# Prefix logsumexp over time: two consecutive steps per partition, result over x, Exp one tile ahead, one table set

## The chip, the core and the metric

The kernel runs on one core of a Trainium2 chip. The core has five engines that run side by side and wait for each other through semaphores: TensorE (PE, matrix products), VectorE (DVE), ScalarE (ACT, functions such as Exp and Ln by tables), GpSimd (POOL) and SyncE (SP). In this kernel SP issues the loads and POOL the stores; all of them run on the same 16 DMA engines. The metric is device time in microseconds, the median of several runs of the same program.

## The reference

```python
def setup_inputs():
    B, S, D = (4, 4096, 4128)
    return {'x': np.random.randn(B, S, D).astype(np.float32)}

def reference(x):
    out[:, 0, :] = x[:, 0, :].copy()
    for t in range(1, S):
        mx = np.maximum(out[:, t - 1, :], x[:, t, :])
        out[:, t, :] = mx + np.log(np.exp(out[:, t - 1, :] - mx) + np.exp(x[:, t, :] - mx))
```

For each of four batches and each of 4128 columns this is a running logsumexp over 4096 time steps: out[t] = ln(exp(x[0]) + ... + exp(x[t])). Input and output are 270.5 MB each in float32.

## The kernel before

The kernel takes Exp of x, sums along time, and takes Ln of the sums. Time lies on the partitions: a tile is 128 consecutive time steps by all 4128 columns, 2.11 MB, and there are 32 tiles per batch, 128 in all. The loop over tiles (lines 54 and 55) is written straight down, and a scheduler sets the order of each engine's instructions from the loop and from the buffers that are free.

For each tile: SP loads xt (line 57; five buffers). ACT writes et = Exp(xt) in float16 (line 60; three buffers). The columns are then worked off in four chunks of 1024 and a tail of 32. For a chunk, PE multiplies et by the upper triangular matrix ut (line 69), which gives the running sums within the tile, in two matmuls of 512 columns; and it adds the running sum of the tiles before with a second pair of matmuls (line 74), whose matrix sel32 has 32 rows and picks the last row of the 32 rows of carry. ACT writes Ln of the sums to ot (line 79; four buffers), and DVE copies the last 32 rows of the sums in float16 to ncarry (line 82), the carry of the next tile. The chunks share three PSUM buffers (pmain); the tail has its own (ptail). POOL stores ot (line 93).

Three things set the order around the change. Each engine runs its instructions in order. The DVE copy of a chunk comes after ACT's Ln of the same chunk, and frees the PSUM buffer. Exp and Ln are taken from two different table sets, so ACT loads a table ahead of each Exp and again ahead of the Ln that follow.

Of the kernel before, what the change touches and what calls it, by code (L numbers as in the profile page):

```python
# [1 line left out]

# [5 lines left out]


@with_exitstack  # L10
def kernel(
    ctx: ExitStack,
    tc: tile.TileContext,
    x: bass.AP,
    out: bass.AP,
):
    nc = tc.nc
    fp32 = mybir.dt.float32
    fp16 = mybir.dt.float16

    B, S, D = x.shape
    P = 128
    n_tt = S // P
    assert S % P == 0

    MAIN = 1024
    MM = 512
    n_main = D // MAIN
    tail = D - n_main * MAIN
    half = (D // 2 + 3) & ~3  # L30

    consts = ctx.enter_context(tc.tile_pool(name="consts", bufs=1))
    ut = consts.tile([P, P], fp16)
    make_upper_triangular(nc, ut, val=1.0, diag=True)
    sel32 = consts.tile([32, P], fp16)
    nc.gpsimd.memset(sel32, 0.0)  # L36
    nc.gpsimd.affine_select(  # L37
        out=sel32, in_=sel32, pattern=[[0, P]],
        compare_op=mybir.AluOpType.not_equal, fill=1.0,
        base=-31, channel_multiplier=1,  # L40
    )

    xpool = ctx.enter_context(tc.tile_pool(name="xpool", bufs=5))
    epool = ctx.enter_context(tc.tile_pool(name="epool", bufs=3))
    opool = ctx.enter_context(tc.tile_pool(name="opool", bufs=4))
    cpool = ctx.enter_context(tc.tile_pool(name="cpool", bufs=3))
    psum_main = ctx.enter_context(tc.tile_pool(name="psum_main", bufs=3, space=bass.MemoryType.PSUM))
    psum_tail = ctx.enter_context(tc.tile_pool(name="psum_tail", bufs=2, space=bass.MemoryType.PSUM))

    carry = [None] * B  # L50

    for b in range(B):
        for k in range(n_tt):
            rows = slice(k * P, (k + 1) * P)

            xt = xpool.tile([P, D], fp32)
            nc.sync.dma_start(out=xt, in_=x[b, rows, :])

            et = epool.tile([P, D], fp16)
            nc.scalar.activation(et, xt, mybir.ActivationFunctionType.Exp)  # L60

            ot = opool.tile([P, D], fp32)
            ncarry = cpool.tile([32, D], fp16)

            def scan_chunk(pt, cols, width):
                for s in range(0, width, MM):
                    w = min(MM, width - s)
                    seg = slice(cols.start + s, cols.start + s + w)
                    nc.tensor.matmul(  # L69
                        pt[:, s:s + w], lhsT=ut, rhs=et[:, seg],  # L70
                        start=True, stop=(k == 0),
                    )
                    if k > 0:
                        nc.tensor.matmul(  # L74
                            pt[:, s:s + w], lhsT=sel32,
                            rhs=carry[b][0:32, seg],
                            start=False, stop=True,
                        )
                nc.scalar.activation(  # L79
                    ot[:, cols], pt[:, :width], mybir.ActivationFunctionType.Ln  # L80
                )
                nc.vector.tensor_copy(ncarry[0:32, cols], pt[96:128, :width])  # L82

            for c in range(n_main):
                pmain = psum_main.tile([P, MAIN], fp32)
                scan_chunk(pmain, slice(c * MAIN, (c + 1) * MAIN), MAIN)
            if tail:
                ptail = psum_tail.tile([P, tail], fp32)
                scan_chunk(ptail, slice(n_main * MAIN, D), tail)

            carry[b] = ncarry

            nc.gpsimd.dma_start(out=out[b, rows, :], in_=ot)  # L93


# [1 line left out]
_INS = ['x']  # L97
_OUTS = [((4, 4096, 4128), 'float32')]


# [23 lines left out]
```

## Time and profile before

| what | value |
|---|---|
| median of 3 runs (lowest to highest) | 1530.63 us (1530.13 to 1531.21) |
| profiled execution, first to last instruction | 1528.0 us |
| difference of that span and the median | 2.6 us |
| busy: ACT, PE, DVE | 1302.7, 1107.2, 620.6 us |
| DMA: bytes, mean rate over the span | 541.52 MB, 354 GB/s |
| of these: read and written by the kernel | 270.53 MB each |

The span runs from the first to the last instruction of one profiled execution; all durations below are from that execution, so a time worked out from them is a span, and stands 2.6 us under the median of the runs. "Busy" is time in which an engine executes; an engine can be busy while another sets the pace. The chain of work that ended last follows, from the last instruction back, what each step waited for. A DMA share is the mean share of time in which the 16 DMA engines had a packet under way, and the rate beside it says what they moved.

### The profile page before, as it was taken

What the parts mean: (1) busy time and instruction counts of PE and PEld (TensorE: products, weight loads), DVE (VectorE), ACT (ScalarE), POOL (GpSimd) and SP (SyncE); (2) the same over time, 40 slices, a digit from 0 to 9 for tenths busy, and PEclk for the clock granted to TensorE, in tenths of its full rate; (3) what the DMA queues carried; (4) which work ended last, traced back from release to release, by engine and by line L of the source; (5) the groups of instructions that cost most, each with busy time, mean ns of one, the idle gap of its engine ahead of it and who ended that gap; (6) DMA issues with size and microseconds to landing.
All of it is one profiled execution on the core that took longest, in us unless ns stands there. A gap on an engine that the chain in (4) does not pass through costs nothing.

```text
span 1528.0 us, 7011 instructions
## 1 busy us (share of the span) xinstructions
PE 1107.2 (72%) x2268; PEld 210.5 (14%) x2268; DVE 620.6 (41%) x640; ACT 1302.7 (85%) x1024; POOL 69.2 (5%) x136
## 2 busy tenths in 40 slices
PE   4767777677677776777767777777677777776776
PEld 1111111111111111111111111111111111111111
DVE  2334443444344433443344334433444344434444
ACT  8988888888988888888888888888889888888884
POOL 0000000000000000000000000000000000000000
PEclk7555555555555555555555555555555555555555
DMA  9999999999999999999999999999999999999945
GB/s 396 432 398 360 351 359 360 355 357 353 381 356 357 353 363 352 358 351 366 357 373 352 366 354 357 347 365 359 355 354 381 353 361 352 360 361 352 341 194 221
DMA packets 36900, 541.52 MB, mean 354 GB/s; under 512 B 4096, under 2 KB 4096, under 8 KB 4096
## 3 DMA queue, kind: packets, MB, share of 16 engines
q1 hardware_dynamic: 18432, 270.54, 53.9%
q0 software_dynamic: 18432, 270.54, 41.3%
q8 instruction: 17, 0.28, 0.1%
q14 instruction: 19, 0.16, 0.0%
HBM read 270.53 MB, written 270.53 MB: 354 GB/s over the span
## 4 chain that ended last, share of the span: by engine, by line
ACT 56%; PE 19%; issue 15%; DVE 10%; DMA 1%; ACTq 0%; DVEq 0%
ACT et L60 30%; ACT L60 11%; DVE ncarry L82 10%; ACT ot L79 10%; PE pmain L69 10%; PE pmain L74 9%; ACT L79 5%; DMA xt<-in_x_dram 1%; ACTq L60 0%; DVEq L119 0%; PE ptail L74 0%
## 5 line engine op out<-in xcount | busy, mean ns | idle before, releaser
L82 DVE CAST ncarry<-pmain 32x1024 f16<-32x1024 f32 x512 | 606.4, 1220 | 900.2 <-ACT ot L79 900.2
L69 PE MATMUL pmain<-et,ut 128*128 128x512 f16 x1024 | 613.6, 603 | 403.5 <-DVE ncarry L82 385.6
L79 ACT ACTIVATE ot<-pmain 128x1024 f32<-128x1024 f32 x512 | 496.6, 1024 | 199.3 <-PE pmain L74 195.1
L74 PE MATMUL pmain<-ncarry,sel 32*128 32x512 f16 x992 | 597.5, 602 | 0.0
L60 ACT ACTIVATE et<-xt 128x4128 f16<-128x4128 f32 x128 | 466.2, 3642 | 7.8 <-DMA xt<-in_x_dram 6.4
L74 PEld LDWEIGHTS <-sel 32*128 32x128 f16 x1116 | 101.0, 99 | 835.7 <-issue 835.7
L69 PEld LDWEIGHTS <-ut 128*128 128x128 f16 x1152 | 109.4, 104 | 471.6 <-issue 469.0
L60 ACT ACT_TABLE_LOAD x128 | 164.2, 1283 | 7.2 <-PE pmain L69 3.1
L79 ACT ACT_TABLE_LOAD x128 | 164.2, 1283 | 2.3
L93 POOL DMA_DIRECT2D out_dram<-ot x128 | 68.1, 532 | 1450.4 <-ACT ot L79 1450.4
L69 PE MATMUL ptail<-et,ut 128*128 128x32 f16 x128 | 26.2, 205 | 7.7 <-ACT et L60 7.7
L74 PE MATMUL ptail<-ncarry,sel 32*128 32x32 f16 x124 | 28.3, 228 | 0.0
L79 ACT ACTIVATE ot<-ptail 128x32 f32<-128x32 f32 x128 | 27.9, 218 | 0.0
L82 DVE CAST ncarry<-ptail 32x32 f16<-32x32 f32 x128 | 23.3, 182 | 0.0
masks.py:66 POOL TENSOR_SCALAR_AFFINE_SELECT ut<-ut 128x128 f16<-128x128 f16 x1 | 0.3, 282 | 0.1
L37 POOL TENSOR_SCALAR_AFFINE_SELECT sel<-sel 32x128 f16<-32x128 f16 x1 | 0.3, 282 | 0.0
masks.py:65 POOL MEMSET ut<- 128x128 f16 x1 | 0.2, 204 | 0.3 <-POOLq L108 0.3
L36 POOL MEMSET sel<- 32x128 f16 x1 | 0.2, 195 | 0.0
L108 POOL MEMSET const-float32-0.0<- 128x1 f32 x1 | 0.1, 103 | 0.2 <-issue 0.2
L108 POOL MEMSET const-bfloat16-1.0<- 128x1 bf16 x1 | 0.1, 106 | 0.0
L108 POOL MEMSET const-uint8-127<- 128x1 uint8 x1 | 0.1, 106 | 0.0
L108 POOL MEMSET const-float32-1.0<- 128x1 f32 x1 | 0.1, 103 | 0.0
## 6 DMA issues: line engine op xcount, KB each, us to landing
xt<-in_x_dram SPq DMA_DIRECT2D x128, 2064.0 KB, 11.3
out_dram<-ot POOLq DMA_DIRECT2D x128, 2064.0 KB, 12.1
```

What stands on the lines that cost most here:

```text
L36: nc.gpsimd.memset(sel32, 0.0)
L37: nc.gpsimd.affine_select(out=sel32, in_=sel32, pattern=[[0, P]], compare_op=mybir.AluOpType.not_equal, fill=1.0, base=-31, channel_multip ...
L60: nc.scalar.activation(et, xt, mybir.ActivationFunctionType.Exp)
L69: nc.tensor.matmul(pt[:, s:s + w], lhsT=ut, rhs=et[:, seg], start=True, stop=(k == 0),)
L74: nc.tensor.matmul(pt[:, s:s + w], lhsT=sel32, rhs=carry[b][0:32, seg], start=False, stop=True,)
L79: nc.scalar.activation(ot[:, cols], pt[:, :width], mybir.ActivationFunctionType.Ln)
L82: nc.vector.tensor_copy(ncarry[0:32, cols], pt[96:128, :width])
L93: nc.gpsimd.dma_start(out=out[b, rows, :], in_=ot)
L108: nc = _bacc.Bacc("TRN2", target_bir_lowering=False, num_devices=1)
```

## The change

A tile is now 256 consecutive time steps: partition p holds the steps 2p and 2p + 1, one after the other, so a tile is 4.23 MB and there are 64. Four 128x128 matrices in float16 take the place of ut and sel32: incl (rows up to and including), excl (rows before), ident, and last (the last row for all). For a chunk, `head` sums for the even steps: incl times the even rows, excl times the odd rows, last times the carry; ACT takes Ln of it. Then `second` adds ident times the odd rows into the same PSUM buffer, which makes it the sum at the odd steps; ACT takes Ln of that, and DVE copies all 128 rows to the carry of this chunk. The order is written out by hand (`manual_schedule`): `second` of chunk c - 1 comes after `head` of chunk c, and Exp of the next tile is issued ahead of the whole scan of a tile. Ln writes its result over x in xt, and the store reads xt; xt has five buffers of twice the size, et two. One table set that has both Exp and Ln is loaded once.

```diff
+    nc.scalar.preload_act_table_set("natural_log_exp_and_others")
...
     xpool = ctx.enter_context(tc.tile_pool(name="xpool", bufs=5))
-    epool = ctx.enter_context(tc.tile_pool(name="epool", bufs=3))
-    opool = ctx.enter_context(tc.tile_pool(name="opool", bufs=4))
-    cpool = ctx.enter_context(tc.tile_pool(name="cpool", bufs=3))
...
+    epool = ctx.enter_context(tc.tile_pool(name="epool", bufs=2))
+    cpool = ctx.enter_context(tc.tile_pool(name="cpool", bufs=1))
+    pmain = ctx.enter_context(tc.tile_pool(name="pmain", bufs=3, space=bass.MemoryType.PSUM))
...
+        def head(c):
+            pt = pmain.tile([P, CH], FP32, name="pt")
+            for s in range(0, CH, MM):
...
+                mm(o, incl, et[:, 0, seg], True, False)
+            for s in range(0, CH, MM):
...
+                mm(o, excl, et[:, 1, seg], False, first)
+            if not first:
+                for s in range(0, CH, MM):
+                    mm(pt[:, s:s + MM], last, carry[c][:, s:s + MM], False, True)
+            nc.scalar.activation(xt[:, 0, c * CH:(c + 1) * CH], pt, ACT.Ln)
+            return pt
...
+        def second(c, pt):
+            for s in range(0, CH, MM):
+                seg = slice(c * CH + s, c * CH + s + MM)
+                mm(pt[:, s:s + MM], ident, et[:, 1, seg], False, True)
+            nc.scalar.activation(xt[:, 1, c * CH:(c + 1) * CH], pt, ACT.Ln)
+            nc.vector.tensor_copy(carry[c], pt)
...
+        for c in range(n_main):
+            pt = head(c)
+            if prev is not None:
+                second(c - 1, prev)
+            prev = pt
...
+        second(n_main - 1, prev)
+        if tail:
+            nc.scalar.activation(xt[:, :, t0:D], qt, ACT.Ln)
+            nc.vector.tensor_copy(carry_t, qt[:, 1, :])
+        nc.gpsimd.dma_start(
+            out=out[b, k * rows:(k + 1) * rows, :].rearrange("(p j) d -> p j d", j=R), in_=xt,
+        )
...
+    for b, k in work:
+        xt = xpool.tile([P, R, D], FP32, name="xt")
+        nc.sync.dma_start(
+            out=xt, in_=x[b, k * rows:(k + 1) * rows, :].rearrange("(p j) d -> p j d", j=R),
+        )
+        et = epool.tile([P, R, D], FP16, name="et")
+        nc.scalar.activation(et, xt, ACT.Exp)
+        if pending is not None:
+            scan(*pending)
+        pending = (b, k, xt, et)
+    scan(*pending)
```

The same on ACT, for one tile in the middle of the program before (waits in brackets name the engine or the DMA whose semaphore is waited for):

```order
L60 ACT_TABLE_LOAD [waits DMAHW4_49]
L60 ACTIVATE et<-xt 128x4128 [waits PE_49]
L79 ACT_TABLE_LOAD
L79 ACTIVATE ot<-pmain 128x1024 [waits PE_49] x3
L79 ACTIVATE ot<-ptail 128x32 [waits DMASW7_49,PE_49,Activation_49]
L79 ACTIVATE ot<-pmain 128x1024 [waits PE_49]
L60 ACT_TABLE_LOAD [waits DMAHW5_49]
```

And for one tile of the program now, from its neighbour's Exp to the end of its scan (line 98 is Ln of `head`, line 105 Ln of `second`, line 124 the tail):

```order
L139 ACTIVATE et<-xt 128x8256 [waits DMAHW2_49]
L98 ACTIVATE xt<-pt 128x1024 [waits PE_49,Activation_49]
L98 ACTIVATE xt<-pt 128x1024 [waits PE_49]
L105 ACTIVATE xt<-pt 128x1024 [waits PE_49]
L98 ACTIVATE xt<-pt 128x1024 [waits PE_49]
L105 ACTIVATE xt<-pt 128x1024 [waits PE_49]
L98 ACTIVATE xt<-pt 128x1024 [waits PE_49]
L105 ACTIVATE xt<-pt 128x1024 [waits PE_49] x2
L124 ACTIVATE xt<-qt 128x2x32
```

The table loads are gone, the Exp is one instruction for two time steps per partition, and the eight Ln alternate between two chunks. The Exp at the top belongs to the tile after the one whose Ln follow.

On PE, a piece of the program before (numbers tell buffers apart; pmain_2328 is one chunk, ut and sel32 are the two matrices):

```order
L69 LDWEIGHTS ut_58
L69 MATMUL pmain_2328<-et_2310,ut_58 128x512 [waits DVE_49]
L74 LDWEIGHTS sel32_63
L74 MATMUL pmain_2328<-ncarry_2273,sel32_63 128x512
L69 LDWEIGHTS ut_58
L69 MATMUL pmain_2328<-et_2310,ut_58 128x512
L74 LDWEIGHTS sel32_63
L74 MATMUL pmain_2328<-ncarry_2273,sel32_63 128x512
```

And of the program now, at the end of `head` of chunk 1 (pt_289), `second` of chunk 0 (pt_281), and the start of `head` of chunk 2 (pt_301):

```order
L80 LDWEIGHTS last_70
L80 MATMUL pt_289<-carry1_91,last_70 128x512
L80 LDWEIGHTS ident_65
L80 MATMUL pt_281<-et_217,ident_65 128x512 [waits Activation_49]
L80 LDWEIGHTS ident_65
L80 MATMUL pt_281<-et_217,ident_65 128x512
L80 LDWEIGHTS incl_59
L80 MATMUL pt_301<-et_217,incl_59 128x512 [waits DVE_49]
L80 LDWEIGHTS incl_59
L80 MATMUL pt_301<-et_217,incl_59 128x512
```

Each matrix now serves two matmuls in a row, each with its own weight load. The matmul of `second` waits for ACT, and what stands behind it on PE waits with it.

## Rows read from the trace of the kernel before

**Rows 1.** Busy time of each engine, share of the span, instructions.
```profile
PE 1107.2 (72%) x2268; PEld 210.5 (14%) x2268; DVE 620.6 (41%) x640; ACT 1302.7 (85%) x1024; POOL 69.2 (5%) x136
```

**Rows 2.** The chain that ended last, shares of the span by line.
```profile
ACT et L60 30%; ACT L60 11%; DVE ncarry L82 10%; ACT ot L79 10%; PE pmain L69 10%; PE pmain L74 9%; ACT L79 5%; DMA xt<-in_x_dram 1%; ACTq L60 0%; DVEq L119 0%; PE ptail L74 0%
```

**Rows 3.** The chain in order of time, one tile: start us, us, what.
```profile
692.58 1.03 ACT ot L79
693.63 1.24 DVE ncarry L82
694.91 0.58 PE pmain L69
...
697.16 1.02 issue
698.18 1.28 ACT L60
699.48 3.64 ACT et L60
...
711.33 3.64 ACT et L60
```

**Rows 4.** Waits of ACT: us in total, times, longest us.
```profile
ACT ot L79 <- PE pmain L74: 195.1, 123, 1.6
...
ACT et L60 <- DMA xt<-in_x_dram: 6.4, 1, 6.4
```

**Rows 5.** Waits of SP's queue, which issues the reads.
```profile
SPq L57 <- ACT et L60: 1374.2, 123, 12.1
```

**Rows 6.** Stretches: busy us (and instructions) per engine, granted clock, DMA share, GB/s.
```profile
core 0: us, PE busy (x) PEld busy (x) DVE busy (x) ACT busy (x) POOL busy (x), PEclk, DMA share, GB/s
0.00:10.00 10.00, 0.00 (x0) 0.11 (x1) 0.00 (x0) 2.84 (x2) 1.07 (x8) 1.00 0.83 317
10.00:100.00 90.00, 60.58 (x128) 12.30 (x128) 32.68 (x35) 83.93 (x63) 3.33 (x6) 0.55 1.00 428
120.00:1430.00 1310.00, 963.27 (x1973) 182.36 (x1972) 538.42 (x556) 1130.01 (x889) 58.97 (x111) 0.50 0.98 359
```

**Rows 7.** Groups of ACT: busy us, mean ns of one | idle before, and releaser.
```profile
L79 ACT ACTIVATE ot<-pmain 128x1024 f32<-128x1024 f32 x512 | 496.6, 1024 | 199.3 <-PE pmain L74 195.1
...
L60 ACT ACTIVATE et<-xt 128x4128 f16<-128x4128 f32 x128 | 466.2, 3642 | 7.8 <-DMA xt<-in_x_dram 6.4
...
L60 ACT ACT_TABLE_LOAD x128 | 164.2, 1283 | 7.2 <-PE pmain L69 3.1
L79 ACT ACT_TABLE_LOAD x128 | 164.2, 1283 | 2.3
```

**Rows 8.** Timeline, two places: start us, us, engine line op, idle before.
```profile
393.46 0.15 PEld L69 LDWEIGHTS <-ut 128*128 128x128 f16 x1 [0.28 <-issue]
393.89 0.15 PEld L69 LDWEIGHTS <-ut 128*128 128x128 f16 x1 [0.28 <-issue]
...
704.43 2.85 ACT L79 ACTIVATE ot<-pmain 128x1024 f32<-128x1024 f32 x3
...
707.82 0.61 PE L69 MATMUL pmain<-et,ut 128*128 128x512 f16 x1
708.36 0.60 PE L74 MATMUL pmain<-ncarry,sel 32*128 32x512 f16 x1
...
709.00 1.02 ACT L79 ACTIVATE ot<-pmain 128x1024 f32<-128x1024 f32 x1 [1.62 <-PE pmain L74]
```

**Rows 9.** Two stretches of 10 us early in the run (columns as in rows 6).
```profile
10.00:20.00 10.00, 3.34 (x9) 1.18 (x9) 3.63 (x4) 9.94 (x8) 0.00 (x0) 0.93 1.01 433
...
40.00:50.00 10.00, 6.65 (x14) 1.26 (x14) 4.25 (x5) 9.94 (x9) 0.53 (x1) 0.50 1.01 434
```

**Rows 10.** From issue to landing, of the tiles of xt and of out.
```profile
DMA to landing us min/median/max: 7.7/11.3/26.0
...
DMA to landing us min/median/max: 6.5/12.1/17.7
```

More of the change, by code (lines that the diff above doesn't have):

```diff
@@ L4, with _constants, tri, ones_where_zero @@
 import concourse.tile as tile
-from concourse import bass_utils, mybir
+from concourse import mybir
 from concourse._compat import with_exitstack
-from concourse.masks import make_upper_triangular
+FP32 = mybir.dt.float32
+FP16 = mybir.dt.float16
+ACT = mybir.ActivationFunctionType
+P = 128
+R = 2
+CH = 1024
+MM = 512
+def _constants(nc, pool):
+    def tri(base, name):
+        t = pool.tile([P, P], FP16, name=name)
+        nc.gpsimd.memset(t, 1.0)
+        nc.gpsimd.affine_select(
+            out=t, in_=t, pattern=[[1, P]], compare_op=mybir.AluOpType.is_ge,
+            fill=0.0, base=base, channel_multiplier=-1,
+        )
+        return t
+    def ones_where_zero(base, mult, step, name):
+        t = pool.tile([P, P], FP16, name=name)
+        nc.gpsimd.memset(t, 0.0)
+        nc.gpsimd.affine_select(
+            out=t, in_=t, pattern=[[step, P]], compare_op=mybir.AluOpType.not_equal,
+            fill=1.0, base=base, channel_multiplier=mult,
+        )
+        return t
+    return (
+        tri(0, "incl"),
+        tri(-1, "excl"),
+        ones_where_zero(0, 1, -1, "ident"),
+        ones_where_zero(-(P - 1), 1, 0, "last"),
+    )
 @with_exitstack
@@ L17 @@
     nc = tc.nc
-    fp32 = mybir.dt.float32
-    fp16 = mybir.dt.float16
     B, S, D = x.shape
[L22 to L30, printed above, removed]
-    consts = ctx.enter_context(tc.tile_pool(name="consts", bufs=1))
[L33 to L41, printed above, removed]
-    xpool = ctx.enter_context(tc.tile_pool(name="xpool", bufs=5))
-    epool = ctx.enter_context(tc.tile_pool(name="epool", bufs=3))
-    opool = ctx.enter_context(tc.tile_pool(name="opool", bufs=4))
-    cpool = ctx.enter_context(tc.tile_pool(name="cpool", bufs=3))
-    psum_main = ctx.enter_context(tc.tile_pool(name="psum_main", bufs=3, space=bass.MemoryType.PSUM))
@@ L48 @@
[L48 to L93, printed above, removed]
@@ new lines @@
+    rows = P * R
+    n_t = S // rows
+    assert S % rows == 0
+    n_main = D // CH
+    tail = D - n_main * CH
+    t0 = n_main * CH
+    nc.scalar.preload_act_table_set("natural_log_exp_and_others")
+    consts = ctx.enter_context(tc.tile_pool(name="consts", bufs=1))
+    incl, excl, ident, last = _constants(nc, consts)
+    xpool = ctx.enter_context(tc.tile_pool(name="xpool", bufs=5))
+    epool = ctx.enter_context(tc.tile_pool(name="epool", bufs=2))
+    cpool = ctx.enter_context(tc.tile_pool(name="cpool", bufs=1))
@@ new lines, with mm, scan @@
+    pmain = ctx.enter_context(tc.tile_pool(name="pmain", bufs=3, space=bass.MemoryType.PSUM))
+    ptail = ctx.enter_context(tc.tile_pool(name="ptail", bufs=2, space=bass.MemoryType.PSUM))
+    carry = [cpool.tile([P, CH], FP16, name=f"carry{c}") for c in range(n_main)]
+    carry_t = cpool.tile([P, tail], FP16, name="carry_t") if tail else None
+    def mm(pt, w, rhs, start, stop):
+        nc.tensor.matmul(pt, lhsT=w, rhs=rhs, start=start, stop=stop, skip_group_check=True)
+    def scan(b, k, xt, et):
+        first = k == 0
+        def head(c):
+            pt = pmain.tile([P, CH], FP32, name="pt")
+            for s in range(0, CH, MM):
+                o = pt[:, s:s + MM]
+                seg = slice(c * CH + s, c * CH + s + MM)
+                mm(o, incl, et[:, 0, seg], True, False)
+            for s in range(0, CH, MM):
+                o = pt[:, s:s + MM]
+                seg = slice(c * CH + s, c * CH + s + MM)
+                mm(o, excl, et[:, 1, seg], False, first)
[6 more added lines that the diff above has]
+            for s in range(0, CH, MM):
+                seg = slice(c * CH + s, c * CH + s + MM)
+                mm(pt[:, s:s + MM], ident, et[:, 1, seg], False, True)
+            nc.scalar.activation(xt[:, 1, c * CH:(c + 1) * CH], pt, ACT.Ln)
+            nc.vector.tensor_copy(carry[c], pt)
+        prev = None
+        for c in range(n_main):
[4 more added lines that the diff above has]
+        if tail:
+            qt = ptail.tile([P, R, tail], FP32, name="qt")
+            seg = slice(t0, D)
+            for j in range(R):
+                mm(qt[:, j, :], incl, et[:, 0, seg], j == 0, False)
+                mm(qt[:, j, :], incl if j else excl, et[:, 1, seg], False, first)
+                if not first:
+                    mm(qt[:, j, :], last, carry_t, False, True)
+        second(n_main - 1, prev)
+        if tail:
+            nc.scalar.activation(xt[:, :, t0:D], qt, ACT.Ln)
+            nc.vector.tensor_copy(carry_t, qt[:, 1, :])
+        nc.gpsimd.dma_start(
+            out=out[b, k * rows:(k + 1) * rows, :].rearrange("(p j) d -> p j d", j=R), in_=xt,
+        )
```

4 lines of the change are left out of this document (added).

## The prediction, made before the changed kernel ran

> **What bounds the kernel now.** I read the busy shares first: ACT 85%, PE 72%, DVE 41% [rows 1]. ACT is the fullest engine but not full, so the next view is the chain that ended last, by line. More than half of it is ACT (the Exp of line 60, its table loads, the Ln of line 79), the rest DVE's carry copy and PE [rows 2]. In order of time it is a ring that closes once per tile: Exp starts at 699.48 and again at 711.33, 11.85 us later. Around it go, one round earlier, the first Ln at 692.58 (1.03 us), the DVE copy that frees that PSUM buffer (1.24), four matmuls for the last chunk (694.91 to 697.16), one more Ln (1.02, under "issue"), a table load (1.28), the Exp (3.64) [rows 3], and behind the Exp a second table load (1283 ns, [rows 7]) before the next Ln. 128 tiles at 11.85 us are 1517 us of a span of 1528.0.
>
> Who waits agrees. In the whole run ACT waited 195.1 us for PE and 6.4 us, once, for a read [rows 4]. The read queue on SP waited 1374.2 us for Exp to free an xt buffer [rows 5]. So input is early and the ring sets the pace.
>
> The DMA row contradicts this at first sight: its share is 0.98 from 120 to 1430 us. But there it moves 359 GB/s, which is just what a ring of 11.85 us asks for (two transfers of 2.11 MB: 4.23 / 11.85 = 357). From 10 to 100 us, when reads were catching up with five buffers and writes had begun, the share was 1.00 and the rate 428 GB/s [rows 6]. The share counts packets in flight, also slow ones; it is no measure of what is left. I take 428 GB/s as the capacity for mixed traffic.
>
> **The change, by its parts, for one new tile of 256 rows (64 of them; two old tiles, 23.7 us).**
>
> *Table loads.* 128 and 128 of 1283 ns, 328 us of ACT, become one, under the first read [rows 7]. All of it was on the ring.
>
> *Exp.* One instruction of 8256 columns. From 1024 columns in 1024 ns and 4128 in 3642 ns [rows 7], a column costs 0.843 ns; 3.64 + 4128 x 0.843 ns = 7.12 us. No row shows Exp and Ln from one table set; the nearest are these two, so I take their durations. The worse bound, twice 3.64, adds 0.16 us per tile; it can matter only where ACT is late.
>
> *Ln.* Eight of 1024 columns instead of eight; back to back they start 0.915 us apart ((2.85 - 1.02) / 2, [rows 8]). The tail's two become one. ACT's own work is 7.12 + 8 x 0.915 + 0.2 = 14.6 us per new tile, against 23.7 now.
>
> *The new ring.* Exp of tile k+1 stands on ACT ahead of the Ln of tile k. Under it PE makes chunks 0 and 1 (12 matmuls, 5.1 us), then stops: the second step's matmul of chunk 0 adds into a buffer that Ln must have read, and chunk 2 stands behind it on PE. So after Exp: one Ln and a hop (1.07 us), 20 matmuls in order, six small ones, then the result reaches ACT 0.21 us after its columns have streamed (a last matmul at 708.36, 0.43 us, Ln at 709.00 [rows 8]), the last Ln (1.02) and the tail's (about 0.12 more). A matmul follows another by 0.43 us where both use the same weights (weight loads at 393.46 and 393.89) and by 0.54 us where 128-row and 32-row weights alternate (707.82, 708.36) [rows 8]. At 0.427: 20 x 0.427 = 8.54, six small at 0.16 = 0.96 by the spacing of the tail's two, sum 1.07 + 8.54 + 0.96 + 0.21 + 1.02 + 0.12 = 11.9 us. With Exp 19.0 us per new tile. DVE's four copies (1.2 us each) lie under this; they free a buffer 2 us before chunk 3 wants it.
>
> *Weights.* Every matrix is now 128 rows, and half of the 20 matmuls change it; the trace has no pair of different 128-row matrices. Bounds: 0.43 and 0.54 us. I take 0.43, since the nearest row in shape, a full load after a full load, has it. If changes cost 0.54, the ring is 20.1 us; if every load does, 21.2. The Trainium skill, "TensorE: Matmul & The Clock Gate", Step-by-step: what each phase is for, says that PE pulls a weight load ahead of running matmuls when the row groups don't conflict or the background buffer takes it; this trace agrees for equal weights (0.43) and not for alternating ones (0.54). By the rule the ring is 19.0 us, by the alternating rows 20.1 to 21.2.
>
> *Clock.* The granted clock is 0.50 (1.2 GHz) nearly everywhere; only the stretch 10 to 20 us has 0.93, in which PE ran its first dense full-weight matmuls [rows 9]. The new order is denser with full weights, so the clock may rise to 2.4 GHz; then 20 matmuls take 4.3 us less and the ring is at most 14.7 to 15 us.
>
> *Transfers.* The same 541.07 MB in half as many DMAs, each 4.227 MB. At 428 GB/s one takes 9.88 us, a read and a write 19.75 us. That is above 19.0: **the transfers become the bound**, and ACT waits for reads.
>
> *One buffer for x and result.* Now a read waits for a write to land, not for Exp. With five buffers, one is held between Exp and Ln, one is written, and reads are queued on the others; nothing is lost as long as the DMA engines always find one queued. The constants (four 128x128 matrices, on POOL) lie under the first read.
>
> *Sum.* By the landing of the last read, 64 reads and some 60 writes have gone: 124 x 9.88 = 1225 us. The first 10 us ran at 317 GB/s instead of 428 [rows 6], 2.6 us lost. After it come Exp (7.1), the scan of the last tile but one (11.9), the last scan (11.9 + 4 for the two chunks that have no Exp to lie under), and a write alone: a 2.11 MB write landed in 6.5 us at best [rows 10], of which 4.94 is the transfer, so 9.88 + 1.56 = 11.4. Sum 1225 + 2.6 + 7.1 + 11.9 + 15.9 + 11.4 = 1274 us. At the higher clock the two scans are some 8 us shorter, 1266. Between them I take 1270. The span of the profiled run is 1528.0 and the median of the runs 1530.63; I add the 2.6 us: **1272 us**.
>
> What rate the mixed traffic sustains decides most. Its ends: 434 GB/s, the best 10 us stretch [rows 9], gives 1247 + 2.6 + 2.6 + some 3 at the ends = 1255; 359 is the rival below.
>
> **The rivals.**
>
> (a) *PE's ring is the bound*, because changes of weights are not hidden and the clock stays low: 64 x 20.1 = 1286 (half exposed) or 64 x 21.2 = 1357 (all), plus 12.6 us to the first landing (2.6 + 9.9), 2.8 for the second tile's read, 11.4 for the last write and 2.6 around: 1316 to 1386. For it: every alternating pair in the trace pays 0.11 us. Against: those loads have 32 rows. 12%.
>
> (b) *Mixed traffic runs below 428* in the long run, since reads that start on an idle engine take longer: the median landing of a single 2.11 MB read is 11.3 us against 7.7 at best [rows 10]. At 400 GB/s: 124 x 10.57 + 49 + 2.6 = 1362. Against: with queued reads no read starts alone. 8%.
>
> (c) *The transfers are at their limit already*: 359 GB/s is the chip's sustained rate and the 428 was a burst of 90 us. Then 124 x 11.77 + 49 + 2.6 = 1511, faster by 1.3% at best. For it: a DMA share of 0.98 for 1300 us. Against: 195.1 us of waits for PE and one for a read [rows 4]. 4%. The Trainium skill, "DMA: Bandwidth & Descriptors", Where 436 GB/s comes from, says that for transfers between HBM and SBUF the HBM side at about 358 GB/s binds, which is this rival; its 541.07 / 358 would be 1511 us for the bytes alone. The trace disagrees: 428 GB/s over 90 us [rows 6].
>
> (d) *Slower: the buffers run out.* Read k+1 lands, Exp k+1 (7.1), scan k behind it (11.9), write k (W), read k+5 (R): a loop of four tiles, T = (19.0 + W + R) / 4. The median landings, 11.3 and 12.1 us [rows 10], doubled for twice the bytes, give T = 16.5, no bound. It becomes slower than now from T = 23.5, that is W + R = 75 us. The longest landings, 26.0 and 17.7 [rows 10], doubled, give T = 26.6 and some 1702 + 29 = 1731 us. They came from queueing at the start, not from a steady state. 2%.
>
> **How the numbers follow.** Forecast (transfers at about 428 GB/s, 1257 to 1290): 72%. (a) 12%, (b) 8%, (c) 4%, (d) 2%, and 2% for less than 1255. The range 1255 to 1345 holds the forecast, the lower part of (a) and half of (b), some 83%. What a measurement can tell from no change is about 0.2%; only (d), and a (c) that comes out worse, are not faster: faster 0.95, same 0.02, slower 0.03.
>
> **What the new profile would show.** If right: one table load; Exp near 7.1 us; a DMA rate of 420 to 434 GB/s throughout; ACT's largest wait at the Exp, for reads; the read queue waiting for writes to land. If weight loads show (a): Ln waits for PE, matmuls of changed weights 0.54 us apart, the DMA rate near 400. If (c): the DMA rate back at 360 with ACT waiting for reads. If (d): the same waits, but gaps in the DMA share. A granted clock of 1.0 would say that the scans are shorter than written here, worth some 8 us at the end. The forecast is wrong if the rate with queued transfers is not 428.

## The result, and the profile after

The changed kernel takes 1271.3 us (median of 4 runs, 1269.8 to 1274.9) against 1530.4 for the kernel before beside it: a ratio of 0.831, 95% interval 0.8298 to 0.8323. The prediction said 1272, range 1255 to 1345.

Busy time and the DMA rate in 40 slices of the span, from the page after; they answer to [rows 1] and [rows 6].

```profile
PE 606.9 (48%) x2392; PEld 241.0 (19%) x2392; DVE 313.8 (25%) x320; ACT 948.6 (75%) x641; POOL 36.0 (3%) x76
...
GB/s 401 430 418 433 434 432 433 433 432 433 432 432 432 433 433 433 432 434 433 433 433 432 433 433 432 432 433 433 434 433 432 433 434 433 432 433 432 432 411 273
```

No engine is full any more: ACT fell from 85% to 75%, PE from 72% to 48%. The rate stands at 432 to 434 GB/s from the fourth slice to the one before the last two. In longer stretches (columns as in [rows 6]):

```profile
10.00:100.00 90.00, 44.22 (x162) 17.22 (x162) 20.79 (x21) 75.83 (x45) 2.28 (x4) 0.80 1.00 425
...
300.00:600.00 300.00, 144.69 (x569) 57.30 (x568) 75.51 (x78) 225.31 (x153) 8.50 (x16) 0.76 1.00 433
...
1225.00:1268.00 43.00, 14.10 (x64) 5.82 (x63) 9.81 (x10) 22.52 (x19) 1.06 (x2) 0.73 0.70 302
```

The DMA share is 1.00, hardly more than the 0.98 of the kernel before at 359 GB/s. What shows that the transfers are now the bound is not the share but who waits: ACT (us in total, times, longest) and the read queue on SP, answering to [rows 4] and [rows 5].

```profile
ACT et L139 <- DMA xt<-in_x_dram: 181.1, 60, 11.1
ACT xt L98 <- PE pt L80: 109.8, 96, 1.5
```

```profile
SPq L135 <- DMA out_dram<-xt: 1174.0, 59, 59.4
```

ACT waits for a read in 60 of 64 tiles, where it waited once before, and reads wait for stores to land, no longer for Exp. One tile on ACT (start us, us, engine line op, idle before):

```profile
695.57 7.08 ACT L139 ACTIVATE et<-xt 128x8256 f16<-128x8256 f32 x1 [2.55 <-DMA xt<-in_x_dram]
702.56 1.92 ACT L98 ACTIVATE xt<-pt 128x1024 f32<-128x1024 f32 x2
704.67 1.02 ACT L105 ACTIVATE xt<-pt 128x1024 f32<-128x1024 f32 x1 [0.18 <-PE pt L80]
707.23 1.02 ACT L98 ACTIVATE xt<-pt 128x1024 f32<-128x1024 f32 x1 [1.54 <-PE pt L80]
708.15 1.02 ACT L105 ACTIVATE xt<-pt 128x1024 f32<-128x1024 f32 x1
709.97 1.02 ACT L98 ACTIVATE xt<-pt 128x1024 f32<-128x1024 f32 x1 [0.81 <-PE pt L80]
710.89 1.94 ACT L105 ACTIVATE xt<-pt 128x1024 f32<-128x1024 f32 x2
712.70 0.24 ACT L124 ACTIVATE xt<-qt 128x64 f32<-128x64 f32 x1
715.21 7.08 ACT L139 ACTIVATE et<-xt 128x8256 f16<-128x8256 f32 x1 [2.27 <-DMA xt<-in_x_dram]
```

There is no table load; in this tile the work from Exp to the tail's Ln takes 17.4 us, and then the engine stands 2.3 us for the next read. The period is 19.6 us, which is 8.454 MB at 431 GB/s. On PE the weight loads tell the spacing of the matmuls of that tile:

```profile
704.00 0.15 PEld L80 LDWEIGHTS <-incl 128*128 128x128 f16 x1 [0.28 <-issue]
704.43 0.15 PEld L80 LDWEIGHTS <-incl 128*128 128x128 f16 x1 [0.28 <-issue]
704.86 0.15 PEld L80 LDWEIGHTS <-excl 128*128 128x128 f16 x1 [0.28 <-issue]
705.28 0.15 PEld L80 LDWEIGHTS <-excl 128*128 128x128 f16 x1 [0.28 <-issue]
...
711.26 0.31 PEld L80 LDWEIGHTS <-incl 128*128 128x128 f16 x2
711.69 0.31 PEld L80 LDWEIGHTS <-excl 128*128 128x128 f16 x2
712.12 0.31 PEld L80 LDWEIGHTS <-last 128*128 128x128 f16 x2
```

The step is 0.43 us whether the matrix changes (incl to excl) or not; later in the scan two matmuls fit in 0.43. The granted clock has gone from 0.50 (1.2 GHz) to 1.00 (2.4 GHz) in between; over the run its mean is 0.76.

The chain that ended last, so useful before [rows 2], says little here: it steps back through POOL's store issues, and calls the rest "issue".

```profile
issue 89%; DMA 6%; POOL 2%; ACT 1%; PE 1%; DVE 0%; POOLq 0%; DVEq 0%; SPq 0%
```

### The profile page after: what moved, and what is told of

The parts are those of the page before. It is cut to its first block, busy times and chain, and to the rows that moved or that the text cites. A ratio compares the mean times of both kernels' runs of the same rounds, so it can differ in the third digit from the quotient of the medians.

```text
span 1268.1 us, 6438 instructions
## 1 busy us (share of the span) xinstructions
PE 606.9 (48%) x2392; PEld 241.0 (19%) x2392; DVE 313.8 (25%) x320; ACT 948.6 (75%) x641; POOL 36.0 (3%) x76
## 4 chain that ended last, share of the span: by engine, by line
issue 89%; DMA 6%; POOL 2%; ACT 1%; PE 1%; DVE 0%; POOLq 0%; DVEq 0%; SPq 0%
DMA xt<-in_x_dram 3%; DMA out_dram<-xt 3%; POOL out_dram L126 2%; PE pt L80 1%; ACT xt L98 0%; ACT xt L105 0%; DVE carry L106 0%; POOLq L126 0%; DVEq L169 0%; DVE carry_t L125 0%; ACT et L139 0%; SPq L135 0%; DVEq L125 0%
## 5 line engine op out<-in xcount | busy, mean ns | idle before, releaser
L139 ACT ACTIVATE et<-xt 128x8256 f16<-128x8256 f32 x64 | 453.4, 7084 | 181.1 <-DMA xt<-in_x_dram 181.1
L106 DVE CAST carry<-pt 128x1024 f16<-128x1024 f32 x256 | 307.5, 1222 | 940.1 <-ACT xt L105 940.1
L80 PE MATMUL pt<-et,ident 128*128 128x512 f16 x512 | 197.3, 475 | 603.2 <-ACT xt L98 603.2
L98 ACT ACTIVATE xt<-pt 128x1024 f32<-128x1024 f32 x256 | 254.4, 1020 | 110.3 <-PE pt L80 109.8
L105 ACT ACTIVATE xt<-pt 128x1024 f32<-128x1024 f32 x256 | 255.0, 1026 | 11.6 <-PE pt L80 11.6
L80 PE MATMUL pt<-et,incl 128*128 128x512 f16 x512 | 192.4, 464 | 41.0 <-DVE carry L106 20.5
L80 PE MATMUL pt<-et,excl 128*128 128x512 f16 x512 | 185.8, 450 | 0.0
L80 PE MATMUL pt<-carry,last 128*128 128x512 f16 x480 | 167.0, 434 | 0.0
L80 PEld LDWEIGHTS <-incl 128*128 128x128 f16 x704 | 73.7, 111 | 153.0 <-issue 116.4
L80 PEld LDWEIGHTS <-excl 128*128 128x128 f16 x576 | 64.5, 112 | 96.2 <-issue 48.9
L80 PEld LDWEIGHTS <-last 128*128 128x128 f16 x600 | 63.4, 108 | 77.7 <-issue 36.8
L126 POOL DMA_DIRECT2D out_dram<-xt x64 | 34.2, 534 | 1216.6 <-ACT xt L124 1216.6
L125 DVE CAST carry_t<-qt 128x32 f16<-128x32 f32 x64 | 11.6, 181 | 0.0
## 6 DMA issues: line engine op xcount, KB each, us to landing
out_dram<-xt POOLq DMA_DIRECT2D x64, 4128.0 KB, 34.2
```

The source lines that it names most:

```text
L80: nc.tensor.matmul(pt, lhsT=w, rhs=rhs, start=start, stop=stop, skip_group_check=True)
L98: nc.scalar.activation(xt[:, 0, c * CH:(c + 1) * CH], pt, ACT.Ln)
L105: nc.scalar.activation(xt[:, 1, c * CH:(c + 1) * CH], pt, ACT.Ln)
L106: nc.vector.tensor_copy(carry[c], pt)
L125: nc.vector.tensor_copy(carry_t, qt[:, 1, :])
L126: nc.gpsimd.dma_start(out=out[b, k * rows:(k + 1) * rows, :].rearrange("(p j) d -> p j d", j=R), in_=xt,)
```

## The experiments

Two questions were open. Is the time really that of the transfers (theory A), or of the loop through ACT and the buffers, which also takes 19.6 us per tile? And which part of the change broke the old ring? All ratios are to the kernel before on the same chip, 1529.7 to 1530.4 us.

**Loads and stores alone** (`copy_only`): Exp, matmuls and Ln left out, so out is x.

```diff
-        et = epool.tile([P, R, D], FP16, name="et")
-        nc.scalar.activation(et, xt, ACT.Exp)
...
+        nc.gpsimd.dma_start(out=out[b, k * rows:(k + 1) * rows, :].rearrange("(p j) d -> p j d", j=R), in_=xt)
```

> The changed kernel's loads and stores alone, with its tiles and its five buffers; nothing is computed, x is stored as it came. Theory A (transfers bind): 541.07 MB at 433 GB/s are 1249.6 us, with 2.6 at the start, some 5 for the last landing and 2.6 around the span: 1257 to 1262 us, so at most 1% under the changed kernel. Theory B (the loop through ACT and the five buffers sets the 19.6 us and the transfers could go faster): clearly under 1240 us.

Measured 1259.0 us (median of 6 runs, 1258.9 to 1274.0), ratio 0.826 (0.823 to 0.829). Its steady stretch (columns here: ACT, POOL, clock, DMA share, GB/s):

```profile
100.00:1100.00 1000.00, 0.00 (x0) 27.10 (x51) 1.00 1.00 433
```

The same 433 GB/s with no compute at all. Theory A holds: by the medians, the changed kernel is within 1% of moving the data and doing nothing.

**Half of the store** (`after_half_store`): the right half of the result is not stored.

```diff
-            out=out[b, k * rows:(k + 1) * rows, :].rearrange("(p j) d -> p j d", j=R), in_=xt,
+            out=out[b, k * rows:(k + 1) * rows, 0:D // 2].rearrange("(p j) d -> p j d", j=R),
+            in_=xt[:, :, 0:D // 2],
```

> The changed kernel with the right half of the columns of the result left out of the store, so 405.8 MB move instead of 541.1. Theory A: the transfers of a tile fall to 14.7 us at 433 GB/s and the compute ring, 17.4 to 18.5 us, takes over: 64 rings, 12.6 to the first landing, 2.8 and some 9 at the end, 1140 to 1210 us, with a DMA rate near 350. Theory B (ACT and PE already set the 19.6 us): 1271 us.

Measured 1115.0 us, ratio 0.729 (0.728 to 0.730). The group of its Exp (durations in ns: lowest, median, highest; then the first and the last start), and two in a row on ACT:

```profile
L140 ACT ACTIVATE et<-xt x64: 7082/7105/7107, 13.1 to 1079.6; 128x8256 f16<-128x8256 f32 x64
```

```profile
755.34 7.11 ACT L140 ACTIVATE et<-xt 128x8256 f16<-128x8256 f32 x1
772.41 7.11 ACT L140 ACTIVATE et<-xt 128x8256 f16<-128x8256 f32 x1
```

With fewer bytes ACT stops waiting for reads and the ring shows itself: 17.1 us in most tiles, 17.0 in the mean of the 62 steps from the second Exp (at 22.9) on. That is the compute limit of this kernel, some 2.5 us per tile under its transfers. The expectation, 1140 to 1210, was too high since it took 17.4 to 18.5 for the ring.

**One table set in the kernel before** (`before_one_set`): a single line.

```diff
+    nc.scalar.preload_act_table_set("natural_log_exp_and_others")
     consts = ctx.enter_context(tc.tile_pool(name="consts", bufs=1))
```

> The kernel before with one edit: the table set with Exp and Ln loaded once, so its 256 table loads go; tiles, order and buffers as before. Theory A (the new time is the transfers' at some 430 GB/s, and any ring under 19.6 us per 8.45 MB reaches it): the old ring of 11.85 us loses 2 x 1.283 and comes to 9.28 us per tile, 18.6 per two tiles, under 19.6, so 1265 to 1290 us, DMA rate near 430, ACT now waiting for reads. Theory B (the two steps per partition and the new order are needed): PE's 16 matmuls at 0.54 us and its wait of 3.06 us for the DVE copy make a ring of 11.6 us that takes over, some 1490 us.

Measured 1280.7 us, ratio 0.837 (0.836 to 0.8385). Two tiles on ACT:

```profile
698.35 3.64 ACT L61 ACTIVATE et<-xt 128x4128 f16<-128x4128 f32 x1 [0.73 <-DMA xt<-in_x_dram]
701.89 2.83 ACT L80 ACTIVATE ot<-pmain 128x1024 f32<-128x1024 f32 x3
704.61 0.21 ACT L80 ACTIVATE ot<-ptail 128x32 f32<-128x32 f32 x1
706.44 1.02 ACT L80 ACTIVATE ot<-pmain 128x1024 f32<-128x1024 f32 x1 [1.63 <-PE pmain L75]
708.22 3.64 ACT L61 ACTIVATE et<-xt 128x4128 f16<-128x4128 f32 x1 [0.75 <-DMA xt<-in_x_dram]
...
1254.25 1.02 ACT L80 ACTIVATE ot<-pmain 128x1024 f32<-128x1024 f32 x1 [1.12 <-PE pmain L75]
1256.40 1.02 ACT L80 ACTIVATE ot<-pmain 128x1024 f32<-128x1024 f32 x1 [1.12 <-PE pmain L75]
```

The period fell from 11.85 to 9.87 us, the last 0.7 of it a wait for a read: the transfers bind here too, at 431 GB/s. One line brings 249.3 of the 259 us. PE's ring of 11.6 us (theory B) did not take over: PE's wait for the DVE copy shrank with the table loads gone, from 385.6 us in all to 134.9, so the 3 us of it per tile were a part of the old ring and not a bound beside it. The last two rows show where this kernel is worse than the changed one: its last tiles run at PE's pace, one chunk in 2.15 us.

**The changed kernel with two table sets** (`after_two_sets`).

```diff
-    nc.scalar.preload_act_table_set("natural_log_exp_and_others")
```

> The changed kernel with one edit undone: no common table set, so a table load ahead of each Exp and ahead of the Ln, 128 in all. Theory A: the new ring is 17.4 us (Exp start to the tail's Ln) and gets 2 x 1.28 us, 20.0 us, just over the transfers' 19.6; 64 x 20.0 and some 27 us at the ends, 1290 to 1315 us, ACT hardly waiting for reads. Theory B (table loads were what the change was about): 128 x 1.283 = 164 us on top, 1435 us.

Measured 1289.9 us, ratio 0.843 (0.842 to 0.844), at the lower edge of theory A's range. The group of its Exp (busy us, mean ns | idle before, releaser; then first and last start), and one ring on ACT:

```profile
L138 ACT ACTIVATE et<-xt 128x8256 f16<-128x8256 f32 x64 | 453.3, 7082 | 14.4 <-DMA xt<-in_x_dram 13.8
```

```profile
L138 ACT ACTIVATE et<-xt x64: 7082/7082/7084, 13.2 to 1244.4; 128x8256 f16<-128x8256 f32 x64
```

```profile
712.04 7.08 ACT L138 ACTIVATE et<-xt 128x8256 f16<-128x8256 f32 x1
719.14 1.28 ACT L97 ACT_TABLE_LOAD   x1
...
731.04 1.28 ACT L138 ACT_TABLE_LOAD   x1
732.34 7.08 ACT L138 ACTIVATE et<-xt 128x8256 f16<-128x8256 f32 x1
```

This ring is 20.3 us; from the second Exp (at 22.9) on they go from 18.3 to 20.4 us, 19.7 in the mean, which is 8.454 MB at 429 GB/s. The transfers alone need 19.5, at 433. The 126 loads are 162 us of ACT, and cost 19 us of time; the others fill what was a wait for reads, 181.1 us in the changed kernel and 13.8 here. So the new tiles and order, too, bring nearly everything without the common set. But a part of this is table loads again: a tile of 256 steps needs two loads where two old tiles needed four. By an estimate from the loads' 1.283 us that alone is 64 x 2.57 = 164 us of the 240; what the new order is worth apart from the tile size was not run. The two parts are not additive: each alone comes within 1% of the changed kernel's rate (431 and 429 GB/s against 433).

**Exp not one tile ahead** (`after_no_ahead`).

```diff
-        if pending is not None:
-            scan(*pending)
-        pending = (b, k, xt, et)
-    scan(*pending)
+        scan(b, k, xt, et)
```

> The changed kernel with Exp of a tile right ahead of its own scan instead of one tile earlier. Theory A: the 12 matmuls of chunks 0 and 1 no longer lie under an Exp: 2.6 to 5.1 us by the clock on top of 17.4, 20.0 to 22.5 us per tile, above the transfers' 19.6: 1310 to 1470 us, DMA rate 375 to 425, Ln waiting for PE. Theory B (transfers bind whatever the order): 1271 us.

Measured 1281.1 us, ratio 0.837 (0.836 to 0.839), under the expected 1310 to 1470. On ACT:

```profile
695.89 7.11 ACT L139 ACTIVATE et<-xt 128x8256 f16<-128x8256 f32 x1
705.85 1.02 ACT L98 ACTIVATE xt<-pt 128x1024 f32<-128x1024 f32 x1 [2.85 <-issue]
...
715.51 7.10 ACT L139 ACTIVATE et<-xt 128x8256 f16<-128x8256 f32 x1
```

```profile
L139 ACT ACTIVATE et<-xt x64: 7082/7104/7105, 13.1 to 1244.1; 128x8256 f16<-128x8256 f32 x64
```

```profile
100.00:1200.00 1100.00, 543.91 (x2115) 216.55 (x2114) 275.71 (x281) 830.88 (x565) 29.84 (x56) 0.76 1.00 433
```

The ring grew from 17.0 to some 19.6 us in the mean; single ones go from 17.5 to 20.05. The lower end of the expectation was missed in the mean, since only the six matmuls of chunk 0 stand bare behind Exp (2.85 us); those of chunk 1 partly lie under the first Ln. ACT waits for a read only once, so this ring happens to equal the transfers' pace, with 433 GB/s in the steady stretch as before. So the Exp one tile ahead is worth 10 us here, at the ends of the run, and is a reserve rather than a gain.

**Three buffers of x instead of five** (`after_bufs3`), the fourth rival made real.

```diff
-    xpool = ctx.enter_context(tc.tile_pool(name="xpool", bufs=5))
+    xpool = ctx.enter_context(tc.tile_pool(name="xpool", bufs=3))
```

> The changed kernel with three buffers of x instead of five. Theory A: landings of 27 and 34 us are time spent queued, and shrink when fewer are queued, down to 11.4 us each; the loop is then 2 T = 17.4 + R + W, T = 20 to 23 us: 1320 to 1480 us, with gaps in the DMA share. Theory B (the five-buffer loop itself sets the pace with landings as they are, 4 T = 17.4 + 27 + 34 = 78, T = 19.6): 2 T = 78, T = 39, some 2500 us. If buffers do not matter: 1271.

Measured 1508.6 us, ratio 0.987 (0.985 to 0.988). Steady stretch, and from issue to landing of reads and stores together:

```profile
100.00:1200.00 1100.00, 452.93 (x1780) 180.12 (x1778) 232.75 (x237) 700.40 (x476) 25.05 (x47) 0.72 0.90 363
```

```profile
DMA to landing us min/median/max: 11.4/14.8/31.0
```

Landings did shrink, from medians of 27.0 (read) and 34.2 (store) with five buffers to 14.7 and 14.8, so those were queueing. 2 T = 17.4 + 14.7 + 14.8 gives T = 23.5; the mean step from Exp to Exp is 23.2 (62 steps from 22.9 to 1464.3). The expected upper end, 1480, was missed because I let landings fall to 11.4; they did so only at best. With three buffers nearly the whole gain is gone.

**Two DMAs per load and per store** (`after_16k_rows`), so rows of 16,512 bytes as before.

```diff
-        nc.sync.dma_start(
-            out=xt, in_=x[b, k * rows:(k + 1) * rows, :].rearrange("(p j) d -> p j d", j=R),
-        )
+        src = x[b, k * rows:(k + 1) * rows, :].rearrange("(p j) d -> p j d", j=R)
+        for j in range(R):
+            nc.sync.dma_start(out=xt[:, j, :], in_=src[:, j, :])
```

(and the store likewise)

> The changed kernel with each load and each store issued as two DMAs, one per time step of a partition, so a row of a transfer is 16,512 bytes as before the change and not 33,024. Theory A: the row size is the reason for 433 GB/s here against 431 in the old kernel with one table set, 0.5%; 1275 to 1280 us. Theory B: the 9 us between those two kernels lie at their ends: 1271.

Measured 1275.5 us, ratio 0.8336 (0.8325 to 0.8347), at 431 GB/s:

```profile
100.00:1100.00 1000.00, 483.32 (x1906) 191.76 (x1905) 249.97 (x255) 751.17 (x508) 53.74 (x102) 0.76 1.01 431
```

Its interval lies just above that of the changed kernel's first run (0.8298 to 0.8323) and overlaps that of its second, below (0.8306 to 0.8330); the steady rate, 431 against 433 GB/s, points the same way. So about 4 of the 9 us between the changed kernel and the one-line version probably go with this; that it is the row size and not the number of DMAs was not tried apart. The rest fits the one-line version's slower end, above, but was not isolated.

**Another end** (`after_short_end`): the last Exp behind the scan before it and in two pieces, the last store in four.

```diff
+        if (b, k) == work[-1]:
+            scan(*pending)
+            for lo, hi in ((0, 2 * CH), (2 * CH, D)):
+                nc.scalar.activation(et[:, :, lo:hi], xt[:, :, lo:hi], ACT.Exp)
+            scan(b, k, xt, et, split=True)
+            continue
...
+            if split and c < n_main - 1:
+                cc = slice(c * CH, (c + 1) * CH)
+                nc.gpsimd.dma_start(out=dst[:, :, cc], in_=xt[:, :, cc])
```

> The changed kernel with another end: the scan of the last tile but one ahead of the last Exp, the last Exp in two pieces, and the last tile's result stored in four pieces as its chunks are done. Theory A: nothing but the end is left to gain; from the last read's landing to the end of the span it takes 41.6 us, in which DMA idles for some 10; 1259 to 1265 us. Theory B: the end is bound by the stores as it is, 1271.

Measured 1268.4 us, ratio 0.8299 (0.8287 to 0.8311); less was gained than the 6 to 12 us expected. To tell it from the changed kernel, both ran again on one chip, with the one-line version.

> The changed kernel once more, to stand beside the version with the other end on one chip: 1269 to 1273 us.

> The version with the other end beside the changed kernel on one chip. If the 3 us seen between them (1271.3 and 1268.4, on two chips) are the shorter end, since the last store is issued 2 us earlier: 1267 to 1270 us, with an interval that lies below the changed kernel's. If they are the chips: 1271.

> The kernel before with the one common table set, beside the changed kernel on one chip: if the 9 us between them are of the kernels, 1280 to 1282 us again.

Measured 1271.0 (ratio 0.8318, 0.8306 to 0.8330), 1268.65 (0.8298, 0.8286 to 0.8309) and 1280.5 us (0.8371, 0.8359 to 0.8382). The other end is lower both times, by 0.2%, with intervals that overlap a little: a lead, not a settled gain. The one-line version is slower by 0.75%, clear of both intervals. The end of the changed kernel, from its second run, shows what there was to win; the fourth row is from the version with the other end, and the last tells how long its last store, a quarter of a tile, took from issue to landing:

```profile
1225.00:1235.00 10.00, 1.58 (x6) 0.53 (x5) 0.51 (x2) 8.84 (x3) 0.00 (x0) 0.78 1.00 429
1235.00:1245.00 10.00, 9.07 (x42) 3.88 (x41) 4.90 (x5) 7.63 (x10) 0.53 (x1) 0.88 0.21 90
1245.00:1255.00 10.00, 4.03 (x23) 1.64 (x21) 4.90 (x5) 6.03 (x8) 0.53 (x1) 0.98 0.99 423
```

```profile
1235.00:1245.00 10.00, 6.51 (x22) 2.53 (x22) 1.59 (x3) 9.60 (x5) 0.63 (x2) 0.83 0.99 426
```

```profile
DMA to landing us min/median/max: 12.4/12.4/12.4
```

From 1235 to 1245 the DMA engines are mostly idle (share 0.21). The new order filled that stretch (0.99), but left the last Exp with no Ln or matmul to lie under, so the last store was issued at 1250.7 instead of 1252.7. And the smaller last store did not land sooner after its issue: 12.4 us for a quarter of a tile, 11.9 for a whole one in the changed kernel. Why is open.

## Why the prediction was right

The forecast rested on one reading: that 428 GB/s over 90 us was the capacity for mixed traffic, and that the old kernel's DMA share of 0.98 was not a limit. Copying alone (433 GB/s) and half the store (ACT no longer waits for reads) both show it. Rival (c), 359 GB/s, is refuted: one core moved 433 GB/s through the steady part of the run. The Trainium skill ("DMA: Bandwidth & Descriptors", Where 436 GB/s comes from) states that the HBM side binds at about 358 GB/s; this trace does not agree for a core that runs alone, and nothing here shows what another core beside it would do.

The terms of the sum:

- *Transfers*: 9.88 us each predicted; 8.454 MB per 19.6 us is 9.8. The last Exp started, on its read, at 1226.5; predicted 1225 + 2.6 = 1227.6. That this is 1 us off is partly luck. Up to then the mean rate was 431 GB/s (row below), so 528.6 MB or 125 transfers had gone: one more than the sum's 124, each some 1% shorter than the sum took it.

```profile
0.00:1226.47 1226.47, 592.79 (x2328) 235.21 (x2329) 303.95 (x310) 926.11 (x622) 34.96 (x74) 0.76 1.00 431
```

- *The end*: the four terms predicted sum to 46.3 us at the low clock and some 8 less at the high one, and the forecast took the middle, 42.3; measured 41.6 (1268.1 - 1226.5). Exp took 7.0, each of the two scans 9.5, and the last store landed 11.9 us after its issue at 1252.7, near the 11.4 of the sum. The last scan, put at 15.9 at the low clock, was the largest miss. The other way, 3.5 us passed between that landing and the end of the span, which the sum did not have.

```profile
1243.23 0.53 POOL L126 DMA_DIRECT2D out_dram<-xt  x1 [19.41 <-ACT xt L124]
1252.71 0.53 POOL L126 DMA_DIRECT2D out_dram<-xt  x1 [8.95 <-ACT xt L124]
```

```profile
DMA to landing us min/median/max: 11.9/11.9/11.9
```

- *Exp*: 7.12 predicted, 7.08 measured. Ln from the common set takes 1.02 us as before.
- *The ring*: 19.0 us at the low clock, 14.7 to 15 at the high one; 17.1 measured in most tiles with half of the store, where nothing else binds. It lies between since the clock changes level within a scan, as in the tile above. The six small matmuls, put at 0.96 us, were far cheaper (from 710.20 to 710.34). In the steady part neither moved the time: both lie under the transfers.
- *Clock*: that it rises came true, but the row read for it was weak. In 10 to 20 us of the kernel before the granted clock is 0.93, yet the weight loads of its longest row of matmuls are 0.43 us apart (12.52 to 14.65), the spacing of 1.2 GHz.
- *Weights*: changed 128-row matrices cost nothing, 0.43 us apart as predicted; rival (a) is out. The rule of the Trainium skill that weight loads are pulled ahead ("TensorE: Matmul & The Clock Gate", Step-by-step: what each phase is for) agrees with these 0.43 us, and not with the 0.54 of the old pairs with a 32-row matrix.
- *Reads that start alone*, rival (b): with five buffers the DMA share is 1.00 from 10 us to the last read, and 433 GB/s needs no correction.
- *Buffers*, rival (d): the loop was right in form. It decides at three buffers, and is no bound at five.

What the prediction did not see is that the change holds more than it needs. It named the table loads as 328 us on the ring, and did not work out that taking 2.57 us off a ring of 11.85 leaves 9.3 and so reaches the transfers by itself.

## What to carry to other kernels

When a change takes a bound away, work out the next bound first and then ask which of its parts are needed to reach it; here one line was worth 249 of 259 us, and the other parts bring 240 without it, by the estimate above most of that by halving the table loads. Read the capacity of the DMA engines from a stretch in which work is queued for them, as at the start of a run, and not from their share of busy time, which stood at 0.98 with a sixth of the rate unused. Where a buffer is held through load, compute and store, write down the loop: here (buffers less one) x T = compute + read + store, less one because a tile is held one step longer between its Exp and its Ln. Take care with the landing times in it: those of five buffers (27.0 and 34.2 us) were queueing, and with three they were 14.7 and 14.8, still above the 11.4 of the best one.

## What the runs showed of the hardware

The rate with queued transfers hardly depends on what computes beside it: 433 GB/s with and without compute; with rows of 16,512 bytes it was 431. Reads alone ran at 433 too (10 to 20 us of the kernel before, [rows 9], ahead of its first store at 23.9); stores alone were not measured. The clock: in the one-line version PE was busy 88% of the time (968 of 1100 us) at a granted clock of 0.50 and matmuls 603 ns long. The second run of that version prints a granted clock of 1.00 with matmuls 604 ns long and the same time, so the length and the spacing of matmuls are the surer sign of the clock. In the changed kernel, busy 48%, the mean granted clock is 0.76. Full 128-row matmuls follow each other there, instead of 128-row and 32-row ones in turn, but the idle times and the order differ as well, and no run takes these apart.
